# A 3x3 convolution with residual: inputs kept resident, image pairs on 128 partitions, and four 64x64 tiles of the matmul array

## The chip, the cores and the metric

The kernel runs on one core of one Trainium2 chip. The metric is the device time of one execution in microseconds, given as the median of several runs. A core has a matmul engine (TensorE, PE in the profile, with its weight loads shown apart as PEld), a vector engine (DVE), a scalar engine (ACT), a general engine (POOL), an engine that here only issues transfers (SP), and 16 DMA engines that all transfers share. Operands of the engines lie in SBUF, an on-chip memory of 128 partitions; matmul results go to PSUM, of which the kernel uses eight buffers of 128 partitions x 512 fp32. "q" after an engine's name means its instruction queue.

## The reference

There are 16 images of 64 channels of 64 x 64 pixels, a 3x3 filter from 64 to 64 channels with zero padding of one pixel, and a residual that is added:

```python
x_pad = np.pad(x, ((0, 0), (0, 0), (pad, pad), (pad, pad)), mode='constant')
for b in range(batch):
    for co in range(c_out):
        for ci in range(c_in):
            for kh in range(k):
                for kw in range(k):
                    output[b, co] += weight[co, ci, kh, kw] * x_pad[b, ci, kh:kh+h, kw:kw+w]
return (output + residual).astype(np.float32)
```

All arrays are fp32. x, residual and the output have 16.78 MB each.

## The kernel before

**Layout.** Viewed as (image, channel) rows of 4096 pixels, two images fill 128 partitions. The kernel goes through eight such pairs (`for i in range(NPAIR)`). A 3x3 filter is nine taps, and each tap is a matmul that contracts over 64 input channels. To use all 128 rows of the array, each image gets a padded buffer `xs` of 66 x 66 pixels in bf16 in which partitions 0 to 63 hold the padded image and partitions 64 to 127 hold the same image two rows further down. One matmul over 128 rows then does the taps of filter row `kh` in its upper half, and for `kh` = 0 also those of filter row 2 in its lower half. Six matmuls per output piece do all nine taps; in three of them the lower 64 rows of weights are zero.

**Weights (L44 to L66).** The weights are loaded as they lie (L50), transposed tap by tap on PE with an identity matrix (L61, L65), and copied by ACT to `wl` in bf16 (L62, L66).

**Loads.** The first pair of x comes as fp32 in two halves on SP's queue (L79, L80). The other seven come on POOL's queue and are cast to bf16 in the transfer (L83), as are all eight pairs of the residual (L87). `xd`, `resb` and `outb` have three buffers each, so a transfer on POOL's queue waits until the buffer it fills has been read out. POOL executes its queue in order.

**Padded copies (L97 to L124).** POOL clears the borders of the six `xs` buffers once. For each image ACT copies into the upper half (L106, L109, L119) and DVE into the lower half (L112, L115, L122). For the first pair these copies also cast.

**Matmuls (L126 to L140).** Each pair is cut into eight pieces (chunks) of 8 rows, 512 pixels. One PSUM buffer holds a chunk of both images: the first image's output is on partitions 0 to 63, the second's on 64 to 127. The two images' matmuls are issued in turn, on different column halves of the array.

**Add and store.** DVE adds the residual (L142) into `outb`. After every second chunk a store of 512 KB is issued, in turn from SP and ACT (L151); the last four chunks of the last pair are stored singly (L147).

There is no order written out beyond this program order. Each engine takes its instructions in it, and waits come from the dependences between tiles and from buffers that come free. Transfers also have their semaphores, which a later transfer may have to wait for.

Of the kernel before, what the change touches and what calls it, by code (L numbers as in the profile page):

```python
# [1 line left out]

# [4 lines left out]

FP32 = mybir.dt.float32
BF16 = mybir.dt.bfloat16  # L10
AF = mybir.ActivationFunctionType


@with_exitstack
def kernel(
    ctx: ExitStack,
    tc: tile.TileContext,
    x: bass.AP,
    weight: bass.AP,
    residual: bass.AP,  # L20
    out: bass.AP,
):
    nc = tc.nc

    B, C, H, W = x.shape
    CO = weight.shape[0]
    K = weight.shape[2]
    assert C == 64 and CO == 64 and K == 3 and H == 64 and W == 64

    P = W + 2  # L30
    PADPIX = P * (H + 2)
    NPIX = H * W
    NPAIR = B // 2
    CHUNK = 512
    NCHUNK = 8

    x_bc = x.rearrange("b c h w -> (b c) (h w)")
    res_bc = residual.rearrange("b c h w -> (b c) (h w)")
    out_bc = out.rearrange("b c h w -> (b c) (h w)")
    w_flat = weight.rearrange("co ci kh kw -> co (ci kh kw)")  # L40

    wpool = ctx.enter_context(tc.tile_pool(name="wpool", bufs=1))

    wl = wpool.tile([128, 6, 64], BF16)  # L44
    nc.vector.memset(wl[:, :, :], 0.0)

    wpad = wpool.tile([64, 192 * 9], FP32)
    nc.vector.memset(wpad[:, 0:576], 0.0)
    nc.vector.memset(wpad[:, 1152:1728], 0.0)
    nc.sync.dma_start(out=wpad[:, 576:1152], in_=w_flat[:, :])  # L50
    wpad3 = wpad.rearrange("p (a b) -> p a b", b=9)

    ident = wpool.tile([64, 64], FP32)
    from concourse.masks import make_identity
    make_identity(nc, ident[:, :])

    psum = ctx.enter_context(tc.tile_pool(name="psum", bufs=8, space=bass.MemoryType.PSUM))

    for j in range(6):
        tp = psum.tile([128, CHUNK], FP32, name="ps")  # L60
        nc.tensor.transpose(out=tp[:, 0:64], in_=wpad3[:, 64:192, j], identity=ident[:, :])  # L61
        nc.scalar.activation(out=wl[0:64, j, :], in_=tp[0:64, 0:64], func=AF.Copy)  # L62
    for kw in range(3):
        bt = psum.tile([128, CHUNK], FP32, name="ps")
        nc.tensor.transpose(out=bt[:, 0:64], in_=wpad3[:, 0:128, 6 + kw], identity=ident[:, :])  # L65
        nc.scalar.activation(out=wl[64:128, kw, :], in_=bt[64:128, 0:64], func=AF.Copy)  # L66

    sbuf = ctx.enter_context(tc.tile_pool(name="sbuf", bufs=3))

    XS_BUFS = 6  # L70
    xs_ring = wpool.tile([128, XS_BUFS, PADPIX], BF16)

    for i in range(NPAIR):
        r0 = 128 * i

        if i == 0:
            xd = sbuf.tile([128, NPIX], FP32, name="xd0", bufs=1)
            SPL = 33 * W
            nc.sync.dma_start(out=xd[:, 0:SPL], in_=x_bc[r0 : r0 + 128, 0:SPL])  # L79
            nc.sync.dma_start(out=xd[:, SPL:NPIX], in_=x_bc[r0 : r0 + 128, SPL:NPIX])  # L80
        else:
            xd = sbuf.tile([128, NPIX], BF16)
            nc.gpsimd.dma_start(out=xd[:, :], in_=x_bc[r0 : r0 + 128, :])  # L83
        xd3 = xd.rearrange("p (h w) -> p h w", w=W)

        resb = sbuf.tile([128, NPIX], BF16)
        nc.gpsimd.dma_start(out=resb[:, :], in_=res_bc[r0 : r0 + 128, :])  # L87

        outb = sbuf.tile([128, NPIX], FP32)

        xs3_h = []
        for half in range(2):
            hl = slice(64 * half, 64 * half + 64)
            xs = xs_ring[:, (2 * i + half) % XS_BUFS, :]
            xs3 = xs.rearrange("p (a b) -> p a b", b=P)
            xs3_h.append(xs3)
            if 2 * i + half < XS_BUFS:  # L97
                nc.gpsimd.memset(xs[0:64, 0:67], 0.0)  # L98
                nc.gpsimd.memset(xs3[0:64, 1:64, 65:66], 0.0)  # L99
                nc.gpsimd.memset(xs3[0:64, 2:65, 0:1], 0.0)  # L100
                nc.gpsimd.memset(xs[0:64, PADPIX - 67 : PADPIX], 0.0)  # L101
                nc.gpsimd.memset(xs3[64:128, 0:63, 0:1], 0.0)  # L102
                nc.gpsimd.memset(xs3[64:128, 0:63, 65:66], 0.0)  # L103
                nc.gpsimd.memset(xs[64:128, 63 * P : PADPIX], 0.0)  # L104
            if i == 0:
                nc.scalar.activation(  # L106
                    out=xs3[0:64, 1:34, 1 : W + 1], in_=xd3[hl, 0:33, :], func=AF.Copy
                )
                nc.scalar.activation(  # L109
                    out=xs3[0:64, 34 : H + 1, 1 : W + 1], in_=xd3[hl, 33:H, :], func=AF.Copy  # L110
                )
                nc.vector.tensor_copy(  # L112
                    out=xs3[64:128, 0:32, 1 : W + 1], in_=xd3[hl, 1:33, :]
                )
                nc.vector.tensor_copy(  # L115
                    out=xs3[64:128, 32 : H - 1, 1 : W + 1], in_=xd3[hl, 33:H, :]
                )
            else:
                nc.scalar.activation(  # L119
                    out=xs3[0:64, 1 : H + 1, 1 : W + 1], in_=xd3[hl, :, :], func=AF.Copy  # L120
                )
                nc.vector.tensor_copy(  # L122
                    out=xs3[64:128, 0 : H - 1, 1 : W + 1], in_=xd3[hl, 1:H, :]
                )  # L124

        for c in range(NCHUNK):  # L126
            ps = psum.tile([128, CHUNK], FP32)
            for j in range(6):
                kh, kw = divmod(j, 3)
                first, last = j == 0, j == 5  # L130
                for half in range(2):
                    rhs = xs3_h[half][:, 8 * c + kh : 8 * c + kh + 8, kw : kw + W]
                    nc.tensor.matmul(  # L133
                        out=ps[64 * half : 64 * half + 64, :],
                        lhsT=wl[:, j, :],
                        rhs=rhs,
                        start=first,
                        stop=last,
                        skip_group_check=True,
                    )  # L140
            sl = slice(CHUNK * c, CHUNK * (c + 1))
            nc.vector.tensor_tensor(  # L142
                out=outb[:, sl], in0=ps[:, :], in1=resb[:, sl], op=mybir.AluOpType.add
            )
            if i == NPAIR - 1 and c >= 4:
                eng = nc.sync if c % 2 == 0 else nc.scalar
                eng.dma_start(out=out_bc[r0 : r0 + 128, sl], in_=outb[:, sl])  # L147
            elif c % 2 == 1:
                ssl = slice(CHUNK * (c - 1), CHUNK * (c + 1))
                eng = nc.sync if (c // 2) % 2 == 0 else nc.scalar  # L150
                eng.dma_start(out=out_bc[r0 : r0 + 128, ssl], in_=outb[:, ssl])  # L151


# [1 line left out]
_INS = ['x', 'weight', 'residual']  # L155
_OUTS = [((16, 64, 64, 64), 'float32')]


# [23 lines left out]
```

## Time and profile before

| | |
|---|---|
| median of 6 runs | 127.57 us (127.09 to 128.41) |
| profiled execution, time | 127.97 us |
| profiled execution, span from first to last instruction | 126.2 us |
| mean granted TensorE clock | 0.973 |
| PE busy | 91.3 us (72%) |
| PE weight loads busy | 55.7 us (44%) |
| DVE busy | 81.7 us (65%) |
| ACT busy | 60.7 us (48%) |
| POOL busy | 20.1 us (16%) |
| HBM read, written | 33.70 MB, 16.78 MB |

The profile is of one execution. Its page has the busy time of each engine, the span cut into 40 slices with the busy share of each slice in tenths, the DMA queues, the chain of work that ended last, the costliest groups of instructions, and the DMA issues with the time to landing. A queue's MB count what its packets write: for a transfer that casts fp32 to bf16, that is half of what is read. q0 is POOL's queue, q1 SP's, q10 ACT's. A group's row names line, engine, operation, output <- inputs, shapes and count, then total busy time and mean ns of one, then the idle time just before and what ended most of it. The rows of the windows view give the stretch, its length, the busy us and count for the engines in the order PE, PEld, DVE, ACT, POOL (or for one line's engines), the granted clock, the DMA share and GB/s. Busy times of pipelined matmuls overlap, so the mean of one is longer than the distance between two.

### The profile page before, as it was taken

To read this page: it belongs to the slowest core of one execution; us is meant where nothing else is said; L and a number is where in the kernel's file an instruction comes from. 1 tells how busy PE (TensorE), PEld (TensorE's weight loads), DVE (VectorE), ACT (ScalarE), POOL (GpSimd) and SP (SyncE) were. 2 spreads that over 40 slices of the span, in tenths; PEclk is the share of its full clock that TensorE was granted. 3 is DMA by queue.
4 is the path that set the end of the run, shared out by engine and by line. 5 is a ranking of instruction groups with operands and counts; after the bars stand their busy time and mean duration, and the time that the engine had idled before them with its cause. 6 is when DMAs were issued, how large, how long until landed. Compare 5 with 4: busy or idle time off the path is not lost.

```text
span 126.2 us, 1891 instructions
## 1 busy us (share of the span) xinstructions
PE 91.3 (72%) x777; PEld 55.7 (44%) x777; DVE 81.7 (65%) x85; ACT 60.7 (48%) x28; POOL 20.1 (16%) x63
## 2 busy tenths in 40 slices
PE   0300001999999999992299999999985799999900
PEld 0300000455445454540146667777753466667500
DVE  4002809449999999202999998998049999455510
ACT  4002309999596692650008999896549800000000
POOL 6999920000003100110000110100001000000000
PEclk9999999999999999999779999999999999999995
DMA  3999999999999999999999999999999999999992
GB/s 87 291 273 297 264 240 210 216 218 223 217 223 344 327 222 286 283 270 291 251 218 219 279 288 280 283 284 279 290 275 274 380 274 280 388 417 416 418 401 77
DMA packets 7433, 34.88 MB, mean 276 GB/s; under 512 B 832, under 2 KB 832, under 8 KB 5376
## 3 DMA queue, kind: packets, MB, share of 16 engines
q0 software_dynamic: 2160, 15.73, 60.0%
q1 hardware_dynamic: 2816, 10.63, 21.9%
q10 hardware_dynamic: 2448, 8.39, 16.9%
q8 instruction: 6, 0.10, 0.3%
q14 instruction: 3, 0.02, 0.0%
HBM read 33.70 MB, written 16.78 MB: 400 GB/s over the span
## 4 chain that ended last, share of the span: by engine, by line
DMA 28%; issue 27%; PE 20%; DVE 15%; ACT 2%; POOL 2%; SPq 1%; POOLq 0%; DVEq 0%
DMA xd<-in_x_dram 28%; PE ps L133 20%; DVE xs_ring L122 8%; DVE outb L142 6%; ACT xs_ring L109 1%; POOL xd L83 1%; POOL resb L87 1%; ACT wl L62 1%; SPq L79 0%; SPq L50 0%; ACT wl L66 0%; DVEq L122 0%; POOLq L87 0%; POOLq L83 0%
## 5 line engine op out<-in xcount | busy, mean ns | idle before, releaser
L133 PE MATMUL ps<-xs_ring,wl 128*64 128x512 bf16 x768 | 89.8, 391 | 8.2 <-DVE outb L142 7.7
L133 PEld LDWEIGHTS <-wl 128*64 128x64 bf16 x768 | 54.5, 111 | 43.1 <-issue 7.7
L119 ACT ACTIVATE xs_ring<-xd 64x4096 bf16<-64x4096 bf16 x14 | 50.7, 3620 | 23.8 <-PE ps L133 14.0
L142 DVE TENSOR_TENSOR outb<-ps,resb 128x512 f32<-128x512 f32 x64 | 40.7, 685 | 10.4 <-PE ps L133 9.1
L122 DVE COPY xs_ring<-xd 64x4032 bf16<-64x4032 bf16 x14 | 31.5, 2252 | 14.2 <-DMA xd<-in_x_dram 13.8
L87 POOL DMA_DIRECT2D resb<-in_residual_dram x8 | 4.4, 547 | 66.9 <-DVE outb L142 66.5
L65 PE MATMUL ps<-ident,wpad 64*128 64x64 f32 x3 | 0.8, 333 | 16.5 <-ACT wl L62 16.5
L112 DVE CAST xs_ring<-xd 64x2048 bf16<-64x2048 f32 x2 | 3.7, 1853 | 9.5 <-DMA xd<-in_x_dram 9.5
L106 ACT ACTIVATE xs_ring<-xd 64x2112 bf16<-64x2112 f32 x2 | 3.9, 1966 | 9.7 <-DMA xd<-in_x_dram 9.7
L65 PEld LDWEIGHTS ps<-ident,wpad 64*128 64x128 f32 x3 | 0.5, 200 | 16.7 <-ACT wl L62 16.7
L115 DVE CAST xs_ring<-xd 64x1984 bf16<-64x1984 f32 x2 | 4.4, 2219 | 3.7 <-DMA xd<-in_x_dram 3.6
L109 ACT ACTIVATE xs_ring<-xd 64x1984 bf16<-64x1984 f32 x2 | 3.7, 1852 | 5.4 <-DMA xd<-in_x_dram 5.4
L83 POOL DMA_DIRECT2D xd<-in_x_dram x7 | 3.7, 532 | 9.0 <-ACT xs_ring L119 9.0
L103 POOL MEMSET xs_ring<- 64x63 bf16 x6 | 4.4, 727 | 0.0
L61 PE MATMUL ps<-ident,wpad 64*128 64x64 f32 x6 | 0.9, 321 | 3.6 <-DMA wpad<-in_weight_dram 3.6
L104 POOL MEMSET xs_ring<- 64x198 bf16 x6 | 3.4, 573 | 0.0
L100 POOL MEMSET xs_ring<- 64x63 bf16 x6 | 3.4, 568 | 0.0
L102 POOL MEMSET xs_ring<- 64x63 bf16 x6 | 3.2, 536 | 0.2
L99 POOL MEMSET xs_ring<- 64x63 bf16 x6 | 3.2, 535 | 0.0
L101 POOL MEMSET xs_ring<- 64x67 bf16 x6 | 2.8, 468 | 0.0
L61 PEld LDWEIGHTS ps<-ident,wpad 64*128 64x128 f32 x6 | 0.8, 203 | 3.6 <-POOL xs_ring L102 3.6
L98 POOL MEMSET xs_ring<- 64x67 bf16 x6 | 1.9, 317 | 0.2
(12 smaller groups left out, 4.6 us busy)
## 6 DMA issues: line engine op xcount, KB each, us to landing
resb<-in_residual_dram POOLq DMA_DIRECT2D x8, 1024.0 KB, 16.0
out_dram<-outb SPq DMA_DIRECT2D x15, 512.0 KB, 12.4
out_dram<-outb ACTq DMA_DIRECT2D x15, 512.0 KB, 12.2
xd<-in_x_dram POOLq DMA_DIRECT2D x7, 1024.0 KB, 19.1
xd<-in_x_dram SPq DMA_DIRECT2D x1, 1056.0 KB, 10.4
xd<-in_x_dram SPq DMA_DIRECT2D x1, 992.0 KB, 17.1
out_dram<-outb SPq DMA_DIRECT2D x2, 256.0 KB, 6.3
out_dram<-outb ACTq DMA_DIRECT2D x2, 256.0 KB, 5.5
```

The costliest lines, as they stand in the source:

```text
L83: nc.gpsimd.dma_start(out=xd[:, :], in_=x_bc[r0 : r0 + 128, :])
L87: nc.gpsimd.dma_start(out=resb[:, :], in_=res_bc[r0 : r0 + 128, :])
L100: nc.gpsimd.memset(xs3[0:64, 2:65, 0:1], 0.0)
L103: nc.gpsimd.memset(xs3[64:128, 0:63, 65:66], 0.0)
L106: nc.scalar.activation(out=xs3[0:64, 1:34, 1 : W + 1], in_=xd3[hl, 0:33, :], func=AF.Copy)
L109: nc.scalar.activation(out=xs3[0:64, 34 : H + 1, 1 : W + 1], in_=xd3[hl, 33:H, :], func=AF.Copy)
L112: nc.vector.tensor_copy(out=xs3[64:128, 0:32, 1 : W + 1], in_=xd3[hl, 1:33, :])
L115: nc.vector.tensor_copy(out=xs3[64:128, 32 : H - 1, 1 : W + 1], in_=xd3[hl, 33:H, :])
L119: nc.scalar.activation(out=xs3[0:64, 1 : H + 1, 1 : W + 1], in_=xd3[hl, :, :], func=AF.Copy)
L122: nc.vector.tensor_copy(out=xs3[64:128, 0 : H - 1, 1 : W + 1], in_=xd3[hl, 1:H, :])
L133: nc.tensor.matmul(out=ps[64 * half : 64 * half + 64, :], lhsT=wl[:, j, :], rhs=rhs, start=first, stop=last, skip_group_check=True,)
L142: nc.vector.tensor_tensor(out=outb[:, sl], in0=ps[:, :], in1=resb[:, sl], op=mybir.AluOpType.add)
```

## The change

**Everything resident.** `xt` has eight buffers of 128 x 4096 in bf16, one per pair, and `ro` eight of 128 x 4096 in fp32 for the residual. All eight x transfers are issued on POOL's queue with the cast, all eight residual transfers on SP's queue without one. The weights come on ACT's queue.

**No padded copies.** The matmuls read `xt` directly. Each of the nine taps is a matmul with 64 rows, and at the image's border it is cut to the pixels that exist. The tap (1, 1), which covers the whole chunk, is first. Nine transposes make the weights for both halves of the partitions (`wdup` holds them twice), and DVE copies them to `wl` in two instructions.

**Four tiles of the array.** Two chunks are worked on together, in two PSUM buffers. For each tap there are four matmuls of 64 rows and 64 columns. For the first chunk (`swap` 0) image 0 goes from partitions 0 to 63 to output partitions 0 to 63, and image 1 from 64 to 127 to 64 to 127. For the second (`swap` 1) the outputs are crosswise: image 0 lands on 64 to 127, image 1 on 0 to 63. The four use the four quarters of the array.

**Add.** The first chunk is added to `ro` in place with one instruction over 128 partitions. The second takes two of 64 partitions each, which read PSUM from the other half and so swap the images back.

**Store.** One store of 2 MB per pair, on SP's queue, after the residual loads in program order.

The core of the diff, with the old loads, copies, matmuls and stores (L68 to L151) taken out:

```diff
+    wdup = pool.tile([64, 2, 576], FP32)
+    ident = pool.tile([64, 64], FP32)
+    ro = [pool.tile([128, NPIX], FP32, name=f"ro{p}") for p in range(NPAIR)]
+    xt = [pool.tile([128, NPIX], BF16, name=f"xt{p}") for p in range(NPAIR)]
+    nc.scalar.dma_start(out=wdup[:, 0, :], in_=w_flat[:, :])
+    for p in range(NPAIR):
+        nc.gpsimd.dma_start(out=xt[p][:, :], in_=x_bc[128 * p : 128 * p + 128, :])
+        if p == 0:
+            make_identity(nc, ident[:, :])
+    for p in range(NPAIR):
+        nc.sync.dma_start(out=ro[p][:, :], in_=res_bc[128 * p : 128 * p + 128, :])
+    nc.vector.tensor_copy(out=wdup[:, 1, :], in_=wdup[:, 0, :])
+    wl = pool.tile([128, 9, 64], BF16)
+    wdup3 = wdup.rearrange("p d (ci t) -> p (d ci) t", t=9)
+    for t0, n in ((0, 8), (8, 1)):
         tp = psum.tile([128, CHUNK], FP32, name="ps")
+        for t in range(t0, t0 + n):
+            nc.tensor.transpose(
+                out=tp[:, 64 * (t - t0) : 64 * (t - t0) + 64], in_=wdup3[:, :, t], identity=ident[:, :]
+            )
+        nc.vector.tensor_copy(
+            out=wl[:, t0 : t0 + n, :], in_=tp[:, 0 : 64 * n].rearrange("p (t c) -> p t c", c=64)
+        )
+    for p in range(NPAIR):
+        x3 = xt[p].rearrange("p (h w) -> p h w", w=W)
+        o = ro[p]
+        for c in range(0, NCHUNK, 2):
+            ps = [psum.tile([128, CHUNK], FP32, name="ps") for _ in range(2)]
+            ps3 = [t.rearrange("p (h w) -> p h w", w=W) for t in ps]
+            for i, (kh, kw) in enumerate(TAPS):
+                xlo, xhi = max(0, 1 - kw), min(W, W + 1 - kw)
+                for swap in range(2):
+                    r0 = ROWS * (c + swap)
+                    ylo = max(0, 1 - kh - r0)
+                    yhi = min(ROWS, H + 1 - kh - r0)
+                    for half in range(2):
+                        hp = slice(64 * half, 64 * half + 64)
+                        to = 64 * (half ^ swap)
+                        nc.tensor.matmul(
+                            out=ps3[swap][to : to + 64, ylo:yhi, xlo:xhi],
+                            lhsT=wl[hp, 3 * kh + kw, :],
+                            rhs=x3[hp, r0 + ylo + kh - 1 : r0 + yhi + kh - 1, xlo + kw - 1 : xhi + kw - 1],
+                            start=i == 0,
+                            stop=i == len(TAPS) - 1,
+                            skip_group_check=True,
+                        )
             sl = slice(CHUNK * c, CHUNK * (c + 1))
+            nc.vector.tensor_tensor(out=o[:, sl], in0=ps[0][:, :], in1=o[:, sl], op=ADD)
+            sl = slice(CHUNK * (c + 1), CHUNK * (c + 2))
+            for half in range(2):
+                hp = slice(64 * half, 64 * half + 64)
+                fr = 64 - 64 * half
+                nc.vector.tensor_tensor(out=o[hp, sl], in0=ps[1][fr : fr + 64, :], in1=o[hp, sl], op=ADD)
+        nc.sync.dma_start(out=out_bc[128 * p : 128 * p + 128, :], in_=o[:, :])
```

More of the change, by code (lines that the diff above doesn't have):

```diff
@@ L7 @@
 from concourse._compat import with_exitstack
+from concourse.masks import make_identity
 FP32 = mybir.dt.float32
 BF16 = mybir.dt.bfloat16
-AF = mybir.ActivationFunctionType
+ADD = mybir.AluOpType.add
 @with_exitstack
@@ L27 @@
     K = weight.shape[2]
-    assert C == 64 and CO == 64 and K == 3 and H == 64 and W == 64
-    P = W + 2
-    PADPIX = P * (H + 2)
+    assert C == 64 and CO == 64 and K == 3 and H == 64 and W == 64 and B == 16
     NPIX = H * W
     NPAIR = B // 2
-    CHUNK = 512
-    NCHUNK = 8
-    x_bc = x.rearrange("b c h w -> (b c) (h w)")
+    ROWS = 8
+    CHUNK = ROWS * W
+    NCHUNK = NPIX // CHUNK
+    TAPS = [(1, 1), (1, 0), (1, 2), (0, 1), (0, 0), (0, 2), (2, 1), (2, 0), (2, 2)]
     res_bc = residual.rearrange("b c h w -> (b c) (h w)")
@@ L39 @@
     out_bc = out.rearrange("b c h w -> (b c) (h w)")
+    x_bc = x.rearrange("b c h w -> (b c) (h w)")
     w_flat = weight.rearrange("co ci kh kw -> co (ci kh kw)")
[L42 to L55, printed above, removed]
-    psum = ctx.enter_context(tc.tile_pool(name="psum", bufs=8, space=bass.MemoryType.PSUM))
-    for j in range(6):
-        tp = psum.tile([128, CHUNK], FP32, name="ps")
-        nc.tensor.transpose(out=tp[:, 0:64], in_=wpad3[:, 64:192, j], identity=ident[:, :])
-        nc.scalar.activation(out=wl[0:64, j, :], in_=tp[0:64, 0:64], func=AF.Copy)
@@ L63 @@
[L63 to L140, printed above, removed]
-            sl = slice(CHUNK * c, CHUNK * (c + 1))
[L142 to L151, printed above, removed]
@@ new lines @@
+    pool = ctx.enter_context(tc.tile_pool(name="pool", bufs=1))
+    psum = ctx.enter_context(tc.tile_pool(name="psum", bufs=8, space=bass.MemoryType.PSUM))
+    wdup = pool.tile([64, 2, 576], FP32)
[7 more added lines that the diff above has]
+            make_identity(nc, ident[:, :])
```

## The prediction

> **What bounds the kernel now.** I read the 40-slice view first, then the DMA queues.
>
> ```profile
> PE   0300001999999999992299999999985799999900
> DMA  3999999999999999999999999999999999999992
> GB/s 87 291 273 297 264 240 210 216 218 223 217 223 344 327 222 286 283 270 291 251 218 219 279 288 280 283 284 279 290 275 274 380 274 280 388 417 416 418 401 77
> q0 software_dynamic: 2160, 15.73, 60.0%
> q1 hardware_dynamic: 2816, 10.63, 21.9%
> q10 hardware_dynamic: 2448, 8.39, 16.9%
> HBM read 33.70 MB, written 16.78 MB: 400 GB/s over the span
> ```
>
> PE (and DVE, 65% busy) has holes; the DMA row has none between the first and the last slice, and the three queues add to 98.8% of the 16 engines. So the kernel is one long transfer. The GB/s row seems to deny it (210 in one place, 417 in another), but it counts packets by the size that lands: q0 casts fp32 to bf16, so 15.73 MB landed are 31.46 MB read. What has to be compared is the larger side of each transfer, here called stream bytes: 31.46 + 10.63 + 8.39 = 50.48 MB. The chain of waits names other things:
>
> ```profile
> DMA 28%; issue 27%; PE 20%; DVE 15%; ACT 2%; POOL 2%; SPq 1%; POOLq 0%; DVEq 0%
> ```
>
> It follows one semaphore at a time and cannot show that a transfer is slow because others share its engines; "issue 27%" is mostly POOL's x and residual transfers in flight. I therefore trust the DMA row and take the stream's rate stage by stage, from the DMA view cut to windows: 5 to 17 us (fp32 and cast loads together), 19 to 31 (cast loads alone), 108 to 120 (stores alone); the columns are packets, MB landed and share of the 16 engines.
>
> ```profile
> q0 software_dynamic: 235, 1.79, 71.4%
> q1 hardware_dynamic: 219, 1.56, 32.3%
> ...
> q0 software_dynamic: 349, 2.60, 103.5%
> ...
> q1 hardware_dynamic: 686, 2.50, 51.1%
> q10 hardware_dynamic: 678, 2.46, 50.5%
> ```
>
> In stream bytes: (2 x 1.79 + 1.56) MB / 12 us = 428 GB/s; 2 x 2.60 / 12 = 433; 4.96 / 12 = 413, or 417 with the 0.04 MB of other queues in that window. From 30 to 45 us, where the first stores join, the same view has 1.93 MB on q0 and 1.05 on each of q1 and q10: (2 x 1.93 + 2.10) / 15 = 397. So loads alone run at 428 to 433, stores alone at 417, and a poor stage is where both mix. The ends come from windows of 1 us, whose last two columns are the DMA share and GB/s:
>
> ```profile
> 123.00:124.00 1.00, 0.00 (x0) 0.00 (x0) 0.00 (x0) 0.00 (x0) 0.00 (x0) 0.50 0.55 209
> 124.00:125.00 1.00, 0.00 (x0) 0.00 (x0) 0.00 (x0) 0.00 (x0) 0.00 (x0) 0.50 0.12 47
> ```
>
> The window from 1 to 2 us has a DMA share of 0.00, that from 2 to 3 is full: the stream starts at 2.0. Counting the two falling rows as (209 + 47) / 417 = 0.6 us of full stream, it ends at 123.6, and 2.6 us follow until the span's end at 126.2. The stream is 121.6 us for 50.48 MB: 415 GB/s on average.
>
> **The change, part by part.**
>
> *Stream bytes: unchanged.* x, residual, weights and output are still 33.70 MB read and 16.78 MB written. Residual is now fp32 in SBUF, twice the bytes landed, but the larger side was fp32 already. No gain, no loss from size.
>
> *Removed work off the stream.* ACT's copies (60.7 us busy), DVE's copies and casts (31.5 + 8.1 us) and POOL's border memsets (most of its 20.1 us) go away. All of it lies under the stream, so I price it at nothing; it would pay only if compute set the end.
>
> *Order of transfers.* All eight x transfers go to POOL's queue and all eight residual loads to SP's, with nothing to wait for; the stores follow behind on SP. That SP's queue serves in order is seen in the two halves of x's first pair, issued 0.6 us apart:
>
> ```profile
> xd<-in_x_dram SPq DMA_DIRECT2D x1, 1056.0 KB, 10.4
> xd<-in_x_dram SPq DMA_DIRECT2D x1, 992.0 KB, 17.1
> ```
>
> Sharing would have landed them together. So stores issued early stay behind the residual loads: loads fill the first part, stores the second. In the mixed window of 5 to 17 us q0 moved 3.58 MB in 16 KB rows and q1 1.56 MB in 8 KB rows, about 2 to 1, so queues alternate row by row; with 16 KB rows on both, x and residual arrive in step, 4.19 MB per pair.
>
> *The loads.* 33.70 MB at 428 (fp32 beside cast, just what the new stage is) are 78.7 us. The ramp: 2 to 19 us moved 6.92 MB, at 428 16.2 us, so 0.8 us was lost at the start; I keep it. Loads run from 2.0 to 81.5. No row shows fp32 loads in 16 KB rows. Bounds: 433, the cast's rate (0.9 us better), and 397, the worst stage (6.2 us worse). I take 428, the nearest row.
>
> *The stores.* 16.78 MB at 417 are 40.2 us. Rows grow from 4 KB to 16 KB: if each row has a fixed price, stores can come up to the 433 of the 16 KB rows of the cast (38.8 us, 1.5 gained); if writing itself is slower, nothing is gained. A single queue in place of two is not shown for stores; POOL's single queue filled all 16 engines with casts (103.5%). Bounds: 1.5 us gained, and 3.4 us lost (43.6 us) at the 385 GB/s that one window of two queues fell to at the end (122 to 123 us). I take 0.5 us gained: 39.7 us, to 121.2.
>
> *The finish.* One store of 2 MB in place of two of 256 KB, but on all engines with a backlog, so I keep 2.6 us: span 123.8. With the 1.8 us outside the span (127.97 - 126.2) this is 125.6 against the profiled execution's 127.97, so 2.4 us less. The median of the runs is 0.4 below that execution: 127.57 - 2.4 = 125.2.
>
> *Does compute stay under it?* The two groups, and the matmul line alone (PE, then PEld) from 100 to 118 us:
>
> ```profile
> L133 PE MATMUL ps<-xs_ring,wl 128*64 128x512 bf16 x768 | 89.8, 391 | 8.2 <-DVE outb L142 7.7
> L142 DVE TENSOR_TENSOR outb<-ps,resb 128x512 f32<-128x512 f32 x64 | 40.7, 685 | 10.4 <-PE ps L133 9.1
> 100.00:118.00 18.00, 18.00 (x168) 12.22 (x166) 1.00 1.03 360
> ```
>
> 168 matmuls in 18 us are 107 ns each, 214 ns for the two that share the array by columns. New: 9 taps x 4 chunk pairs = 36 groups of four 64x64 matmuls per image pair; at 214 ns a group (all four at once) 7.7 us. DVE: 4 whole adds and 8 half-height ones; height does not shorten a vector operation as far as this trace shows, so 12 x 0.685 = 8.2 us (bounds for a crosswise half: 0.34 to 1.37 us, giving 5.5 to 13.7 us). A pair arrives every 4.19 MB / 428 = 9.8 us, so compute waits for data: pair 0 lands near 13, the last near 82, last add near 91. Its store is the eighth in line and its turn comes at 123.8 - 2.6 - 5.0 = 116. Cover: (116 - 13) / 8 = 12.9 us per pair. Compute decides only above that, which is 358 ns per group of four, or 1.27 us per half add. POOL's eight issues (0.53 us each) and SP's eight (about 0.5 us) end by 6 us; the weight path (nine transposes of 0.3 us, two DVE copies) ends well before pair 0 lands, otherwise each us late eats cover, not time. On SP a store waits for DVE's adds, and behind it stand only later pairs' stores, which need later adds anyway. A store can also be held for an earlier transfer, as now:
>
> ```profile
> SPq L151 <- DMA out_dram<-outb: 12.0, 4, 4.7
> ```
>
> The earlier ones are then residual loads, landed by that time; nothing.
>
> **A rule against it.** The row shows two matmuls at once in one bank (ps), on different column halves, both using all 128 rows. Splitting rows as well is not in this trace. The Trainium skill, TensorEngine Tiling (Array Packing), Restrictions and Gotchas, says that tiles on different rows cannot access one PSUM bank at the same time. In the new order the first two matmuls of a group are on different rows and write the same bank, in different partitions. Taken literally the four go in two rounds, 428 ns a group, 15.4 us per pair, over the cover: 13 + 8 x 15.4 = 136, then the last add, 5.0 us for the last store and 2.6: span about 145, time 146. By the row, where sharing a bank in different partitions costs nothing, 214 ns and no effect. I go with the row, since both cases share a bank by disjoint partitions.
>
> **Rivals.**
> 1. *Nothing gained.* The stream goes on at its average of 415: 50.48 MB again 121.6 us, same ends: time 127.6 on the median's scale. For it: bytes are equal. Against it: full queues from the start, and unmixed stages at 417 to 433.
> 2. *PE becomes the bound (the slower side).* Place: the four-matmul group. Price: 36 x 8 = 288 groups; from 358 ns on, each 10 ns more adds 2.9 us; at 428 ns 146 us. Four weight loads per group instead of two could do the same: one takes 111 ns, and if no two overlapped they would be 444 ns. Against it: in 100 to 118 us 166 loads were busy for only 12.2 us, 74 ns apiece, so they do overlap.
> 3. *Big rows on one queue are slower.* Stores at 385 and loads at 410: 43.6 + 82.2 us, span 131.2, time 132.6.
>
> **Chances and range.** Forecast (faster, 123.3 to 126.9) 0.68; rival 1 0.12; rival 2 0.11; rival 3, with lesser forms that end just above 128.2, 0.09. "Within 0.5%", about what the runs can tell from no change, is 126.9 to 128.2. The low end is all good bounds together (0.9 + 1.0 beyond what I took, 123.3, and 0.3 of the ramp); the high end takes in the lesser half of rival 3 and leaves out rival 2: 123.0 to 129.5.
>
> **What would show it.** Right: DMA row full throughout; SP's queue loading until about 81 us and storing after; loads near 428, stores near 417 to 425; first matmul near 13 us; last add near 91 us, with PE idle in each 9.8 us. Wrong: PE busy without gaps to beyond 110 us, DMA below full in the second half (rival 2); or a full DMA row at under 410 GB/s of stream bytes (rivals 1 and 3); or last x landing after 100 us, which would mean that the queues do not share row by row.

## The result and the profile after

The changed kernel takes **126.68 us** (median of 18 runs, 125.92 to 127.09) against 127.54 for the kernel before (39 runs). The ratio is 0.992 with a 95% interval of 0.990 to 0.994: faster by 0.8%. The forecast was 125.2 us, 1.9% faster. The direction is the forecast one and the time lies in the stated range, but the gain is 0.9 us where 2.4 was forecast.

The profiled execution took 127.01 us with a span of 125.1. Its page, in the lines that answer to those shown of before:

```profile
PE   0003079989949949948967976999990000000000
DMA  5999999999999999999999999999999999999960
GB/s 105 364 327 309 346 306 293 338 335 296 317 346 314 306 338 301 322 343 304 301 351 325 299 333 335 293 335 414 424 440 429 435 424 429 429 435 440 424 288 10
q1 hardware_dynamic: 2304, 33.56, 64.1%
q0 software_dynamic: 1152, 8.39, 32.0%
q8 instruction: 9, 0.15, 0.4%
```

The DMA row is full from the second slice to the last but two. Loads fill the first 27 slices and stores the rest, as the order of SP's queue demands. PE has gaps through the load stage and has nothing left to do after slice 30. So the kernel is still one transfer, and PE is hidden under it. The line q8 looks negligible; it turns out to matter. In the kernel before it read:

```profile
q8 instruction: 6, 0.10, 0.3%
```

Two stages of the stream, from the DMA view: 12 to 82 us (loads) and 92 to 112 us (stores).

```profile
q0 software_dynamic: 1019, 7.43, 50.8%
q1 hardware_dynamic: 1018, 14.84, 50.6%
q8 instruction: 7, 0.11, 0.6%
...
q1 hardware_dynamic: 587, 8.54, 99.8%
```

Loads: (2 x 7.43 + 14.84 + 0.11) / 70 = 426 GB/s of stream bytes, where 428 was assumed. Stores: 8.54 / 20 = 427 GB/s, where 39.7 us, that is 423, was assumed. The length of the stream is near the forecast. Its end is not. Windows of 1 us (columns: length, PE, PEld, DVE, POOL, granted clock, DMA share, GB/s):

```profile
119.00:120.00 1.00, 0.00 (x0) 0.00 (x0) 0.00 (x0) 0.00 (x0) 0.50 0.99 426
120.00:121.00 1.00, 0.00 (x0) 0.00 (x0) 0.00 (x0) 0.00 (x0) 0.50 0.69 295
121.00:122.00 1.00, 0.00 (x0) 0.00 (x0) 0.00 (x0) 0.00 (x0) 0.50 0.27 115
122.00:123.00 1.00, 0.00 (x0) 0.00 (x0) 0.00 (x0) 0.00 (x0) 0.50 0.08 33
```

Counted as in the prediction, the stream ends at 120 + (295 + 115 + 33) / 428 = 121.0 us; 121.2 was forecast. But the span goes on for 4.1 us, not 2.6. The last of these rows shows how: a DMA share of 0.08 is about one engine of sixteen still at work.

The trace records the small packet with which each of the 16 engines reports its part of a transfer. The table has the last one of each engine. (The kernel before ends with several small stores on two queues; there each engine's packets, which follow one another almost without a gap, are followed to its last one.)

```
kernel   q8 fetches   median engine   mean engine   last engine   last - median   span
before        6           123.53         123.64        124.76          1.23       126.2
after         9           121.36         121.36        123.47          2.11       125.1
```

The mean engine finishes 2.3 us earlier than before, close to the forecast gain of 2.4. The last engine finishes only 1.3 us earlier, and the kernel ends with the last engine. A further 0.2 us is lost between the last part and the end of the span (1.43 us before, 1.67 after).

### The profile page after: what moved, and what is told of

The parts are those of the page before. It is cut to its first block, busy times and chain, and to the rows that moved or that the text cites. A ratio compares the mean times of both kernels' runs of the same rounds, so it can differ in the third digit from the quotient of the medians.

```text
span 125.1 us, 2518 instructions
## 1 busy us (share of the span) xinstructions
PE 69.0 (55%) x1161; PEld 57.3 (46%) x1161; DVE 67.5 (54%) x99; POOL 4.9 (4%) x14
## 3 DMA queue, kind: packets, MB, share of 16 engines
q1 hardware_dynamic: 2304, 33.56, 64.1%
HBM read 33.70 MB, written 16.78 MB: 403 GB/s over the span
## 4 chain that ended last, share of the span: by engine, by line
DMA 35%; PE 23%; DVE 11%; another core or an unknown queue 4%; POOL 1%; issue 1%; DVEq 1%; POOLq 0%
DMA xt<-in_x_dram 35%; PE ps L91 23%; DVE ro L105 7%; DVE ro L100 3%; POOL xt L54 1%; DVEq L132 1%; POOL ident masks.py:199 0%; POOL ident masks.py:197 0%; POOLq masks.py:199 0%; POOLq L121 0%
## 5 line engine op out<-in xcount | busy, mean ns | idle before, releaser
L91 PE MATMUL ps<-xt,wl 64*64 64x504 bf16 (+3 forms) x1152 | 67.8, 394 | 13.5 <-DMA xt<-in_x_dram 13.5
L91 PEld LDWEIGHTS <-wl 64*64 64x64 bf16 x1152 | 56.2, 112 | 24.8 <-DMA xt<-in_x_dram 12.8
L105 DVE TENSOR_TENSOR ro<-ps,ro 64x512 f32<-64x512 f32 x64 | 44.0, 688 | 1.3
L100 DVE TENSOR_TENSOR ro<-ps,ro 128x512 f32<-128x512 f32 x32 | 22.1, 692 | 15.9 <-PE ps L91 15.2
L67 PE MATMUL ps<-ident,wdup 64*128 64x64 f32 x9 | 1.3, 320 | 11.4 <-DVE wdup L61 11.4
L67 PEld LDWEIGHTS ps<-ident,wdup 64*128 64x128 f32 x9 | 1.1, 205 | 11.4 <-issue 11.4
L61 DVE COPY wdup<-wdup 64x576 f32<-64x576 f32 x1 | 0.5, 453 | 10.9 <-DMA wdup<-in_weight_dram 10.9
L54 POOL DMA_DIRECT2D xt<-in_x_dram x8 | 4.4, 585 | 0.8 <-POOLq L121 0.8
L70 DVE CAST wl<-ps 128x512 bf16<-128x512 f32 (+1 forms) x2 | 0.8, 453 | 1.3 <-PE ps L67 1.3
## 6 DMA issues: line engine op xcount, KB each, us to landing
wdup<-in_weight_dram ACTq DMA_DIRECT2D x1, 144.0 KB, 10.1
```

Source lines behind the costliest of these rows:

```text
L54: nc.gpsimd.dma_start(out=xt[p][:, :], in_=x_bc[128 * p : 128 * p + 128, :])
L61: nc.vector.tensor_copy(out=wdup[:, 1, :], in_=wdup[:, 0, :])
L67: nc.tensor.transpose(out=tp[:, 64 * (t - t0) : 64 * (t - t0) + 64], in_=wdup3[:, :, t], identity=ident[:, :])
L70: nc.vector.tensor_copy(out=wl[:, t0 : t0 + n, :], in_=tp[:, 0 : 64 * n].rearrange("p (t c) -> p t c", c=64))
L91: nc.tensor.matmul(out=ps3[swap][to : to + 64, ylo:yhi, xlo:xhi], lhsT=wl[hp, 3 * kh + kw, :], rhs=x3[hp, r0 + ylo + kh - 1 : r0 + yhi + k ...
L100: nc.vector.tensor_tensor(out=o[:, sl], in0=ps[0][:, :], in1=o[:, sl], op=ADD)
```

## The experiments

**Theory A.** Packets of q8 fetch PE's instructions. Each is 16 KB and takes 0.93 us on one DMA engine. A transfer gives each engine a fixed sixteenth, and the queues are filled far ahead, so an engine that has served a fetch stays late until the end. In the trace of after, from store to store:

```
store (of 8)   median part   last - median
   2               92.07          0.90
                   (a q8 packet starts at 93.6)
   3               97.05          2.11
   4 to 8      101.91 to 121.36   2.11
```

In this stage an engine's packets follow one another without a gap, so that one engine can be followed. The engine that served the fetch at 93.59 us had reported the last part of store 2, at 92.98. Its next part came 6.18 us later; with no fetch the distance is 4.86. The fetch and a slow packet behind it (974 ns, where 611 is usual) cost it 1.3 us, and it ends last, at 123.47.

**Theory B.** The lag belongs to the large stores and rows on one queue, whatever PE does. **Theory C.** It comes with compute as such.

### Only the stream

```diff
     for p in range(NPAIR):
-        x3 = xt[p].rearrange("p (h w) -> p h w", w=W)
         o = ro[p]
-        for c in range(0, NCHUNK, 2):
-...
         nc.sync.dma_start(out=out_bc[128 * p : 128 * p + 128, :], in_=o[:, :])
```

> The kernel after without its convolution and its adds: x, residual and weights are loaded and each residual pair is stored as it came, on the same queues; the output is the residual alone. PE has almost no instructions left, so none has to be fetched during the stream. Theory A (the 2.1 us by which the last DMA engine ends behind the median one come from PE's nine instruction fetches of 16 KB, each 0.93 us on a single engine, which the fixed shares of a transfer never even out): the last store's 16 parts end within 0.6 us of their median, the median comes about 0.5 us earlier (120.9 us), span near 122.9, time near 124.8. Theory B (the lag belongs to 16 KB rows or 2 MB stores on one queue, whatever PE does): the last part still ends 1.5 to 2.1 us after the median, span 124.6 or more, time 126.3 or more.

It took 124.50 us (124.29 to 124.51; ratio 0.975, 0.973 to 0.978). Its page has no line q8, and the windows at its end read:

```profile
119.00:120.00 1.00, 0.00 (x0) 0.00 (x0) 0.00 (x0) 0.00 (x0) 1.00 0.99 426
120.00:121.00 1.00, 0.00 (x0) 0.00 (x0) 0.00 (x0) 0.00 (x0) 1.00 0.31 131
121.00:122.00 1.00, 0.00 (x0) 0.00 (x0) 0.00 (x0) 0.00 (x0) 1.00 0.00 0
```

All engines end within 0.8 us of each other. The last part is 0.46 us behind the median, and that distance is the same at every one of the 16 transfers of SP's queue. The runs of this kernel also lie within 0.2 us, those of after within 1.2. B falls. This says that the convolution and its adds cost the stream 2.2 us although PE is idle for almost half of the span; whether it does so by fetches or otherwise is for the next runs.

### Five taps

```diff
-            for i, (kh, kw) in enumerate(TAPS):
+            for i, (kh, kw) in enumerate(TAPS[0:5]):
...
-                            stop=i == len(TAPS) - 1,
+                            stop=i == 4,
```

> The kernel after with five of the nine taps, so the output lacks four taps of the filter: 1280 instructions of PE for the convolution and 5 fetches in place of 9. Theory A: the mean over the 16 engines comes 0.2 to 0.35 us earlier, the last engine lags by 1.1 us or less behind the median: span 123.7 to 124.2, time 125.5 to 126.0. Rival C (the lag comes with compute as such: matmuls and adds that use SBUF and PSUM beside the stream): four taps fewer leave the adds and half of the matmuls, time 126.4 or more.

125.44 us (ratio 0.983, 0.981 to 0.986), span 123.7. The DMA part of its page:

```profile
q1 hardware_dynamic: 2304, 33.56, 64.9%
q0 software_dynamic: 1152, 8.39, 32.4%
q10 hardware_dynamic: 80, 0.15, 0.3%
q8 instruction: 5, 0.08, 0.2%
```

The mean part comes at 121.04, 0.3 us earlier than in after, and the last at 122.04. The shift of the mean is that of theory A, and the time is just under its 125.5 to 126.0. The lag of 1.29 us behind the median is over the 1.1 expected: ten engines ended within 0.4 us of each other and six later, so the median is one of the early ones; behind the mean the lag is 1.0. All adds are kept and C expected 126.4 or more, so C falls as the main cause.

### Twice the instructions

```diff
-                        nc.tensor.matmul(
-                            out=ps3[swap][to : to + 64, ylo:yhi, xlo:xhi],
+                        ym = (ylo + yhi) // 2
+                        for ya, yb in ((ylo, ym), (ym, yhi)):
+                            nc.tensor.matmul(
+                                out=ps3[swap][to : to + 64, ya:yb, xlo:xhi],
...
-                            start=i == 0,
+                                start=i == 0 and ya == ylo,
```

> The kernel after with every matmul cut into two of half the rows, so that PE has twice the instructions (4608 in place of 2304) and about 18 fetches in place of 9; the transfers and the result are the same. Theory A: 9 more fetches are 8.4 us of engine time, 0.5 us on the mean of 16 engines, and the last engine lags by 2 to 3 us: span 125.6 to 126.6, time 127.2 to 128.2, if a pair's matmuls stay under 12.9 us. Theory B: no change, 126.7 within 0.3.

It took 139.04 us (ratio 1.088, 1.084 to 1.092). There were 18 fetches, as expected, but the time is 11 us beyond what either theory said. The waits of this kernel, then the DMA row of its page (40 slices of 3.4 us) and PE's order of time show why (columns of the last: start, us, what, and the idle time before it):

```profile
PEld L93 <- issue: 40.9, 17, 3.3
PE ps L93 <- issue: 33.7, 16, 3.1
```

```profile
DMA  5999999999999999999999999999999960590093
...
32.40 3.71 PE L93 MATMUL ps<-xt,wl 64*64 64x256 bf16 x128 [1.19 <-issue]
39.14 5.36 PE L93 MATMUL ps<-xt,wl 64*64 64x252 bf16 x128 [3.04 <-issue]
45.88 3.71 PE L93 MATMUL ps<-xt,wl 64*64 64x252 bf16 x128 [1.38 <-issue]
51.80 3.70 PE L93 MATMUL ps<-xt,wl 64*64 64x256 bf16 x128 [2.22 <-issue]
...
114.58 8.85 PE L93 MATMUL ps<-xt,wl 64*64 64x189 bf16 x256 [2.50 <-issue]
```

Up to 114 us PE stops after every 128 matmuls. With their weight loads these are 256 instructions, and that is what one packet of q8 brings: 4608 / 256 = 18 packets here, 2304 / 256 = 9 in after, 1280 / 256 = 5 with five taps, and 1536 / 256 = 6 in the kernel before. PE starves for its own program, for 1.2 to 3.0 us in the first four rows. Beside the stream a fetch started 3.5 to 4.5 us after PE began a block, and PE went on 1.2 to 1.6 us after the fetch had ended. The last row shows what the stream has to do with it: around 115 us the DMA engines were almost idle, the fetch started 1.15 us after the block, at 115.73, and PE ran through 256 matmuls without a stop. With the stops a pair takes longer than its cover, and PE becomes the bound. The stream before that point still follows A: the sixth store's mean part is at 110.89 with no fetch, 111.64 with nine in all, 112.13 with the fourteen served by then in this run, 0.08 to 0.09 us for each. The 1.3 us that one engine lost above are 0.08 on the mean of 16.

### Small stores

```diff
-        nc.sync.dma_start(out=out_bc[128 * p : 128 * p + 128, :], in_=o[:, :])
+            ssl = slice(CHUNK * c, CHUNK * (c + 2))
+            nc.sync.dma_start(out=out_bc[128 * p : 128 * p + 128, ssl], in_=o[:, ssl])
```

> The kernel after with each 2 MB store cut into four of 512 KB, rows of 4 KB, all on SP's queue behind the residual loads. If a row has a fixed price, the stores go back from 431 to about 417 GB/s, 1.3 us more over 16.78 MB: time 128.0, with the lag of the last engine as it was (theory A). Theory B (coarse rows make the lag): the lag falls to the 1.0 us of the kernel before and takes back 1.1 of the 1.3 us: time 126.9.

128.05 us (ratio 1.004, 1.002 to 1.006). From 92 to 112 us the DMA view reads:

```profile
DMA packets 2303, 8.39 MB, mean 419 GB/s; under 512 B 255, under 2 KB 255, under 8 KB 2303
q1 hardware_dynamic: 2303, 8.39, 102.6%
```

That is 419 GB/s against 427 in after. The last engine lags by 2.2 us behind the median, as in after, and not by the 1.0 of theory B. Small stores have a price of their own, and large ones are worth 1.4 us here (128.05 - 126.68); the edit changes the row and the number of transfers together, so which of the two costs is not set apart. The run also shows that without them the new kernel is slightly slower than the old one: what the order of transfers brings to the mean engine is lost at the last one.

### The start

```diff
-    for p in range(NPAIR):
-        nc.sync.dma_start(out=ro[p][:, :], in_=res_bc[128 * p : 128 * p + 128, :])
+    nc.sync.dma_start(out=ro[0][:, :], in_=res_bc[0:128, :])
     nc.vector.tensor_copy(out=wdup[:, 1, :], in_=wdup[:, 0, :])
+    for p in range(1, NPAIR):
+        nc.vector.tensor_copy(out=ro[p][0:64, 0:1], in_=wdup[:, 1, 0:1])
+        nc.sync.dma_start(out=ro[p][:, :], in_=res_bc[128 * p : 128 * p + 128, :])
```

> The kernel after with the residual loads of pairs 1 to 7 held on SP until DVE has copied the weights, so that SP does not issue eight transfers at once. Start theory: SP's burst keeps the other queues from starting (x's first packet came at 5.9 us, the weights landed at 10.1 us after issue): x starts near 3.6 us, the weights land within 4 us, the 2-to-5 us stretch runs at a full DMA share, and the time falls by up to 0.8 us, to about 125.9. Rival: the ramp is what the engines need in any case, as in the kernel before: 126.7 within 0.3.

126.31 us (ratio 0.990, 0.987 to 0.992; that of after is 0.990 to 0.994). The start theory falls: x's first packet still comes at 5.6 us and the weights land 10.1 us after issue, though SP had issued one transfer only. The 0.4 us it gained, a little more than the 0.3 that the rival allowed, are not set apart from the spread of after, and its last engine lags by 1.65 us instead of 2.11. Why the other queues start only at about 5 us when SP's rows are 16 KB stays open.

### Without the crosswise half

```diff
-                        to = 64 * (half ^ swap)
+                        to = 64 * half
...
-            for half in range(2):
-                hp = slice(64 * half, 64 * half + 64)
-                fr = 64 - 64 * half
-                nc.vector.tensor_tensor(out=o[hp, sl], in0=ps[1][fr : fr + 64, :], in1=o[hp, sl], op=ADD)
+            nc.vector.tensor_tensor(out=o[:, sl], in0=ps[1][:, :], in1=o[:, sl], op=ADD)
```

> The kernel after with the second chunk of each two produced straight (image 0 on partitions 0 to 63 of the output, image 1 on 64 to 127) and added with one instruction over 128 partitions, so that only two quarters of the array are ever used. The result is the same. If the four matmuls of a group overlap because they are on four different quarters, a group now takes two rounds, 428 ns, 15.4 us per pair, above the 12.9 us of cover: time 146 within 3. If matmuls on one quarter overlap as well, or the cover is larger than I worked out: 126.7 to 135.

152.83 us (ratio 1.197, 1.192 to 1.201). First the matmul line of after in two windows of a pair each, then the page of this kernel:

```profile
46.00:55.00 9.00, 7.89 (x144) 6.50 (x144) 1.00 1.03 325
56.00:65.00 9.00, 7.89 (x144) 6.50 (x144) 1.00 1.01 316
```

```profile
DMA  5999999999999999999999999999319100930084
...
L91 PE MATMUL ps<-xt,wl 64*64 64x504 bf16 (+3 forms) x1152 | 124.9, 377 | 2.9 <-DMA xt<-in_x_dram 2.9
```

After: 7.89 us / 36 = 219 ns per group of four. Not crosswise: 124.9 / 288 = 434 ns, two rounds. So the crosswise half is what makes the four matmuls overlap, and the holes in the DMA row show PE as the bound. The price is that of rival 2, two rounds, but for another reason: here each quarter has two matmuls in turn. The span of 149.9 us is 5 over the 145 of the prediction: PE began at 16.3 us, not 13 (3.3 us), and a group took 434, not 428 ns (1.6 us). The 146 within 3 expected for the time is missed for the same reasons.

### Fewer instructions for the same result

Two chunks of eight, and in a second run four, are done with the weights of both images on the diagonal of a 128 x 128 array, one matmul in place of two:

```diff
+    wlb = pool.tile([128, 9, 128], BF16)
+    nc.vector.memset(wlb[:, :, :], 0.0)
+    for half in range(2):
+        hp = slice(64 * half, 64 * half + 64)
+        nc.vector.tensor_copy(out=wlb[hp, :, 64 * half : 64 * half + 64], in_=wl[hp, :, :])
...
+                    if c >= NCHUNK - 2:
+                        nc.tensor.matmul(
+                            out=ps3[swap][:, ylo:yhi, xlo:xhi],
+                            lhsT=wlb[:, 3 * kh + kw, :],
+                            rhs=x3[:, r0 + ylo + kh - 1 : r0 + yhi + kh - 1, xlo + kw - 1 : xhi + kw - 1],
...
+            if c >= NCHUNK - 2:
+                nc.vector.tensor_tensor(out=o[:, sl], in0=ps[1][:, :], in1=o[:, sl], op=ADD)
+                continue
```

> The kernel after with the last two of each pair's eight chunks done by matmuls over the whole array, with the weights of both images on the diagonal of 128 x 128: 2016 instructions of PE for the convolution in place of 2304, the same result. A pair's matmuls should take 27 x 219 + 18 x 214 ns = 9.8 us, under the cover. Theory A with the fetches going round about eight engines (the last lag in the kernel after grew from 0.9 to 2.1 us with the ninth fetch): at most 8 fetches, lag 1.2 us or less, time 125.6 to 126.0. If a fetch hits any engine by chance: 126.4 on average, with runs spread as before.

> As the run before it, with four of each pair's eight chunks over the whole array: 1728 instructions of PE, 7 fetches; a pair's matmuls take 18 x 219 + 36 x 214 ns = 11.6 us, still under the 12.9 us of cover. Theory A: mean 0.15 us earlier than the kernel after, lag 1.2 us or less, time 125.4 to 125.9. If the cover is smaller than worked out, the last store is late and the time above 126.7.

125.69 us (ratio 0.985, 0.982 to 0.987) with two chunks and 125.61 (0.985, 0.982 to 0.987) with four. The line of after, then of the run with two chunks, from its page and from windows at its end:

```profile
PE 69.0 (55%) x1161; PEld 57.3 (46%) x1161; DVE 67.5 (54%) x99; POOL 4.9 (4%) x14
...
PE 82.2 (66%) x1009; PEld 54.8 (44%) x1017; DVE 62.7 (51%) x94; POOL 4.9 (4%) x14
...
q8 instruction: 8, 0.13, 0.4%
```

```profile
120.00:121.00 1.00, 0.00 (x0) 0.00 (x0) 0.00 (x0) 0.00 (x0) 0.50 0.65 279
121.00:122.00 1.00, 0.00 (x0) 0.00 (x0) 0.00 (x0) 0.00 (x0) 0.50 0.35 147
122.00:123.00 1.00, 0.00 (x0) 0.00 (x0) 0.00 (x0) 0.00 (x0) 0.50 0.00 0
```

PE works 13 us longer than in after and the kernel is 1.0 us faster, with one fetch fewer. The row from 122 to 123 us, where one engine was left over in after, is empty. All changed kernels that ran to the end on the stream's bound:

```
kernel                PE instructions*   fetches    mean eng.    last eng.  last - mean    time
only the stream                0            0       120.62       121.04        0.42      124.50
five taps                   1280            5       121.04       122.04        1.00      125.44
4 of 8 on full array        1728            7       121.22       122.23        1.01      125.61
2 of 8 on full array        2016            8       121.33       122.24        0.91      125.69
the start                   2304            9       121.20       122.72        1.52      126.31
after                       2304            9       121.36       123.47        2.11      126.68
small stores                2304            9       122.37       124.62        2.25      128.05
* weight loads and matmuls of the convolution
```

Against the stream alone the mean is 0.42 us later with five fetches, 0.60 with seven, 0.71 with eight and 0.74 with nine in after: 0.08 to 0.09 us for each, which leaves next to nothing for the matmuls and adds themselves. (The start has another beginning, and small stores have another rate.) That the loss comes from PE's fetches is thus shown by taking them away: with all compute, with some of it, and with the whole computation kept.

The last engine is about 1 us behind the mean with five, seven and eight fetches and 1.5 to 2.3 us with nine. In after the ninth met an engine that was the last already, as shown above; in the start the ninth, at 89.19 us, cost its engine 1.3 us and made it the last. The lengths of the fetches hint at the reason. In after they are 967, 968, 947, 886, 879, 934, 931, 926 and then 965 ns; with twice the instructions the third to seventh took 934, 931, 928, 969 and 960, the eleventh to fifteenth 934, 931, 925, 968 and 967. A period of eight fits fetches that go round eight engines, so that the ninth meets the first one's again. The records do not name the engine, so this last step is argued and not shown.

## Why the prediction was right or wrong

- **What bounds the kernel, right.** The DMA row was full, and the kernel without compute (124.50) is within 2.5% of both kernels.
- **Order and alternation of queues, right.** Residual loads landed every 9.8 us from 10.7 us on and x's pairs 4.9 us after each, in step row by row. The prediction missed that x is half a pair behind: pair 0 was there at 16 us, not at 13. The cover was (116 - 16.3) / 8 = 12.5 us per pair, not 12.9. It was not needed.
- **Loads, right** (428 assumed, 426 measured). **Stores, faster than taken**: stores 5 to 8 came 4.86 us apart, 431 GB/s, so that 16.78 MB take 38.9 us and not 39.7. Small stores cost 1.4 us more in the experiment, so the gain is near the upper bound of 1.5; 0.5 was taken.
- **The stream's end, right in part by luck**: 121.0 against 121.2. The stores gave 0.8 us more than forecast, and the nine fetches, priced at nothing, took 0.7 us from the mean engine (121.36 against 120.62 in the stream alone). The two misses nearly cancel.
- **The finish, wrong; this is the step that failed.** "On all engines with a backlog, so I keep 2.6 us" took the span from the mean engine's end. It was 4.1 us, and these 1.5 us are what the forecast lacks. A backlog on every engine does not bring them in together: in the stream alone the 16 parts kept their distances through 110 us, and in after an engine once 2.11 us late stayed so from store 3 to store 8. The instruction fetches were in the profile as q8 and were not priced; the change raised them from six to nine, since its 64-row matmuls are more in number. Each made one engine about 1.3 us late, and the ninth fell on the last one: the last engine is 2.11 us behind the mean, where it was 1.12 before.
- **Two matmuls, four matmuls, right.** A group of four takes 219 ns (214 assumed). The rule of the Trainium skill, TensorEngine Tiling (Array Packing), Restrictions and Gotchas, that tiles on different rows cannot use one PSUM bank at the same time, did not bind in this case, where they write different partitions of the bank: the four overlap fully. The measurement decides. When both chunks are straight, each quarter gets two matmuls in turn, and the time doubles.
- **Crosswise adds, right.** A half add took 688 ns, as a whole one does (692). The trace of before has no such pair, so "height does not shorten a vector operation" was an assumption there; the page of after shows it:

```profile
L105 DVE TENSOR_TENSOR ro<-ps,ro 64x512 f32<-64x512 f32 x64 | 44.0, 688 | 1.3
L100 DVE TENSOR_TENSOR ro<-ps,ro 128x512 f32<-128x512 f32 x32 | 22.1, 692 | 15.9 <-PE ps L91 15.2
```

- **Rivals.** Rival 1 (nothing gained) is nearer in time than the forecast's own figure but for another reason: the stream did get shorter. Rival 2 did not occur; two experiments made PE the bound, by two rounds of matmuls (152.83) and by starving PE of instructions (139.04). Rival 3 did not occur: a single queue with large rows stored faster (427 to 431 GB/s) than two with small ones (417).

## What to carry to other kernels

When a kernel is bound by one stream over all DMA engines, its end is set by the slowest engine, so look at how the DMA share falls in the last microseconds and not only at the mean rate. Count PE's instructions too: each 256 here cost a 16 KB fetch that made one engine about 1.3 us late, so fewer and larger matmuls paid even where they kept PE busy longer. Large stores, 2 MB in rows of 16 KB, were the surest gain of this change.

## What was not expected of the hardware

- PE's program comes over the same DMA engines as the data, 256 instructions (16 KB, 0.93 us of one engine) at a time. With the queues full and twice the instructions, PE waited 1.2 to 3.0 us for a block (in the rows shown) when it used one up in 3.7 to 5.4 us; with the engines almost idle, at 115.73 us, it did not wait.
- A transfer issued at 0.75 us on ACT's queue sent its first bytes at 5.1 us, and x's first packet, issued at 1.24 us, came at 5.9, while SP's 16 KB rows ran; in the kernel before, POOL's first transfer, issued at 1.27 us, had its first packet at 3.6. With SP's other transfers held back these were 4.7 and 5.6.
- A distance between engines, once there, stays: in the stream without compute the 16 parts kept the same distances, 0.46 us at most behind the median, for 110 us.
